# First feed-forward product of a transformer block: one 512-column matmul for two 256-column ones in five of seven block products

## The chip, the cores and the metric

The kernel runs on one core of one Trainium2 chip. A core has TensorE (PE: matmuls, which write to the accumulator memory PSUM), VectorE (DVE), ScalarE (ACT), GpSimd (POOL) and SyncE (SP, which here issues the DMA transfers). Each engine works through its own instructions in order, and semaphores make one wait for another. The metric is the device time of one execution in microseconds (us). Differences under about 0.2% can't be told from none.

## The reference, cut to what matters

One layer: a mixed attention block (8 stick-breaking and 8 forgetting heads), then a feed-forward block with a squared ReLU. 512 tokens, model width 2048, feed-forward width 8192, all float32.

```python
x = x + jnp.einsum('bse,ed->bsd', mixed, w_out[l])

h2 = rmsnorm(x, g_mlp[l])
u = jax.nn.relu(jnp.einsum('bsd,df->bsf', h2, w_up[l]))
x = x + jnp.einsum('bsf,fd->bsd', u * u, w_down[l])
return rmsnorm(x, g_final)
```

The change is in the first of the two feed-forward products, `h2 @ w_up`.

## The kernel before, in words

**Precision.** TensorE multiplies in a reduced float32 form (`fp32r` in the profile). To get full precision every operand is split into a high and a low part (`split`, L69 to L76: ScalarE casts the high part, VectorE subtracts it from the source to get the low part), and a product is three matmuls that add up in PSUM (`mm3`, L103): high x high, high x low, low x high.

**Seven products in place of eight.** The large products are done by Strassen's scheme in Winograd's form: both operands are cut in two by two blocks, and seven products of sums of blocks (numbered 1 to 7) replace eight. For the first feed-forward product the left operand is the normalised residual, whose seven sums are made once and kept in SBUF as `F[p]` (high and low part of each; `f_parts`, L507, gives the two parts of chunk `a`, each 128 x 256: 128 of the inner dimension by 256 tokens). In one tile of `F` the high part lies 4 x 256 elements ahead of the low part.

**Units.** `w_up` is worked through in 32 units of 256 columns (`NU` = 32; class `Unit`, L536). A unit loads its two halves of the rows, 1 MB each (`load`, L548, tag `rw`). For each product `parts` (L554) makes the sum of weight blocks that this product needs (one VectorE subtraction over 128x1024 for products 5, 6, 4, 7: L557 to L563) and splits it into `hi` and `lo`. The buffers for these (`hi_lo`, L80) go round: three from one pool and one more in this stage, so at most four products' weights are held. `multiply` (L568) runs over 8 chunks `a` (order `PAIRS`): three matmuls of 128x128 stationary weights and 256 moving columns each, 24 a product and 168 a unit.

**Accumulators.** A unit has three PSUM tiles, `A`, `B`, `C` (`psa`, `psb`, `psc` in the profile), each of the size of a bank, 512 columns, of which it uses 256, in two sets that the units use in turn. Products 1, 6, 7 and 4 add up in `A` one after the other, 5 and 3 in `C`, 2 is alone in `B`. After 1, 6 and 7 ScalarE copies `A` to SBUF (`m`, L592), and VectorE adds such a copy and `B` or `C` into a quarter of the hidden tile `c` (L598 after 7, L600 after 2, L604 after 3); after 4 ScalarE copies `A` straight into `c` (L602). After 3 the whole `c` goes through Relu and Square (L605, L606).

**Order.** Units 0 and 1 are run product by product at the end of the stage before (L886 to L906). For the rest the loop at L925 interleaves the new unit with the products 4 and 3 of the one before:

```python
        for i, (who, p) in enumerate(((new, 1), (old, 4), (new, 5), (new, 6), (old, 3), (new, 2), (new, 7))):
            if who is None:
                continue
            who.product(p)
            if todo and i in (0, 2, 4, 5):
                store_form(*todo.pop(0))
```

`store_form` (L797) makes one of the seven sums of the hidden values of two units, splits it (tile `st`) and stores it to DRAM (`ufd`): seven of them for each pair of units. They are the left operand of the second feed-forward product (`second`, L840; tile `accd`), which runs 512-column matmuls. A scheduler, which estimates times when the program is built, decides from this order and the dependencies how instructions stand on each engine. In the built program before, TensorE runs 6, 2 and 7 of a unit, then 1 of the next, then 4 of the old one, then 5 of the next.

Of the kernel before, what the change touches and what calls it, by code (L numbers as in the profile page):

```python
# [8 lines left out]
F32 = mybir.dt.float32  # L9
F32R = mybir.dt.float32r  # L10
AF = mybir.ActivationFunctionType
ALU = mybir.AluOpType
PSUM = bass.MemoryType.PSUM

P = 128
NT = 512
# [19 lines left out]
def block_kernel(ctx, tc, x, g_attn, w_in, b_f, g_out_sb, g_out_fox, w_out, g_mlp, w_up, w_down, g_final, y):  # L36
    nc = tc.nc
    pe, act, dve, pool, sp = nc.tensor, nc.scalar, nc.vector, nc.gpsimd, nc.sync
# [64 lines left out]
    def mm3(out, sh, sl, mh, ml, first, last):  # L103
        pe.matmul(out, sh, mh, start=first, stop=False, skip_group_check=True)  # L104
        pe.matmul(out, sh, ml, start=False, stop=False, skip_group_check=True)  # L105
        return pe.matmul(out, sl, mh, start=False, stop=last, skip_group_check=True)  # L106
# [59 lines left out]
    with tc.tile_pool(name="att", bufs=1, side="right", reuse_waits="tile") as at:  # L166
# [15 lines left out]
        def accumulate_v(c0, m, steps, prepare=None, more=None, pool_=None):  # L182

            per = NT // m
            banks = [(acc if pool_ is None else pool_).tile([P, NT], F32, tag="acc", name="accv")
                     for _ in range(2 if more is not None else TB // per)]
            if more is not None:
                banks += [more.tile([P, NT], F32, tag="more", name="accm") for _ in range(2)]
            ps = [banks[t // per][:, t % per * m:(t % per + 1) * m] for t in range(TB)]
            k1 = 0  # L190
            for step in steps:
                k0, k1 = k1, k1 + step
                if prepare is not None:
                    prepare(k0, step)
                w = load_w([w_in[k0 * P:(k0 + step) * P, c:c + m // len(c0)].rearrange("(a p) c -> p a c", p=P) for c in c0],
                           step, m)
                for t in range(TB):
                    ts = slice(t * P, (t + 1) * P)
                    for i in range(step):
                        k = k0 + i  # L200
                        mm3(ps[t], hH[k][:, ts], hL[k][:, ts], *w[i], k == 0 and t % per == 0, k == KC - 1)
            return ps
# [126 lines left out]
        def v_columns(h):  # L329
            return 2 * WSB + h * P if h < NH else o0 + 2 * WSB + (h - NH) * P  # L330

        with tc.tile_pool(name="tr0", bufs=2, space=PSUM) as trp:
# [36 lines left out]
            ps = accumulate_v([v_columns(order[0])], 2 * P + NH, [1, 1] + [2] * 7, prepare, trp)  # L369
# [25 lines left out]
        with tc.tile_pool(name="attp", bufs=1, space=PSUM, reuse_waits="tile") as atp:  # L395
# [18 lines left out]
            for t in range(TB):  # L414
                for i in range(t + 1):
                    pe.matmul(cps[:, t, :], utri if i == t else onesr, lf[:, i, :], start=(t == 0 and i == 0),
                              stop=(i == t), skip_group_check=True)
# [32 lines left out]
            for n in range(0, 2 * NH, 2):  # L450
# [15 lines left out]
                if n == 2 * NH - 2:  # L466
                    ps = accumulate_v([v_columns(order[n])], 2 * P, [4] * 4, pool_=accs[1])
                    with tc.high_priority():
                        vs = take_v(ps)
                elif n % 4 == 2:  # L470
                    c = [v_columns(order[n + i]) for i in (0, 2)]
# [33 lines left out]
    F = {p: [None, None] for p in A_ORDER}  # L505

    def f_parts(p, a):  # L507

        t_ = F[p][a // 2 % 2]
        return [t_[:, c, a // 4 * 2 + a % 2, :] for c in range(2)]  # L510


    PAIRS = (0, 1, 4, 5, 6, 7, 2, 3)
# [22 lines left out]
    class Unit:  # L536
        def __init__(self, u):
            self.u = u
            cols = slice(2 * u * P, 2 * (u + 1) * P)
            rows_ = w_up.rearrange("(a i p) f -> i p a f", i=2, p=P)  # L540
            self.rows = rows_[0][:, :, cols], rows_[1][:, :, cols]
            self.b = []
            if u >= 2:
                self.load(0)
                self.load(1)
            self.A = None

        def load(self, i, a=slice(0, KC // 2)):  # L548
            if a.start == 0:
                self.raw = rw.tile([P, KC // 2, 2 * P], F32, tag="rw", name="wu")  # L550
                self.b.append([self.raw[:, :, j * P:(j + 1) * P] for j in range(2)])
            sp.dma_start(self.raw[:, a], self.rows[i][:, a])
# [15 lines left out]
        def multiply(self, p, parts):  # L568
            hi, lo = parts
            if self.A is None:  # L570
                self.A, self.C, self.B = (ups.tile([P, NT], F32, tag=c, name=f"ps{c}")[:, :2 * P] for c in "acb")
            ps = {1: self.A, 6: self.A, 7: self.A, 4: self.A, 2: self.B, 5: self.C, 3: self.C}[p]
            for a in PAIRS:
                ins = mm3(ps, hi[:, a, :], lo[:, a, :], *f_parts(p, a), a == PAIRS[0] and p in (1, 2, 5), a == PAIRS[-1])
            return ins

        def product(self, p):
            ins = self.multiply(p, self.parts(p))
            self.finish(p)
            return ins  # L580

        def finish(self, p):
            if p == 2:
                if self.u % 2 == 0:
                    hidden[0] = (sg[0].tile([P, 2, 2, NT], F32, tag="c", name="c", bufs=2) if self.u else
                                 rw.tile([P, 2, 2, NT], F32, tag="rw", name="c"))
                self.pair = hidden[0]
                self.c = hidden[0][:, self.u % 2]
            t1, t2 = slice(0, 2 * P), slice(2 * P, NT)
            if p in (1, 6, 7):  # L590
                self.m = sm.tile([P, 2 * P], F32, tag="m6" if p == 6 else "m", name=f"s{p}", bufs=2 if p == 6 else 1)
                act.copy(self.m, self.A)  # L592
                if p == 6:
                    self.m6 = self.m
                if p == 1:
                    self.m1 = self.m
            if p == 7:
                dve.tensor_tensor(self.c[:, 1, t2], self.m, self.C, op=ALU.add)  # L598
            if p == 2:
                dve.tensor_tensor(self.c[:, 0, t1], self.m1, self.B, op=ALU.add)  # L600
            if p == 4:
                act.copy(self.c[:, 0, t2], self.A)  # L602
            if p == 3:
                dve.tensor_tensor(self.c[:, 1, t1], self.m6, self.C, op=ALU.add)  # L604
                act.activation(self.c, self.c, AF.Relu)  # L605
                act.activation(self.c, self.c, AF.Square)  # L606
# [19 lines left out]
    def out_piece(p, db, m0):  # L626

        hi, lo = (w.rearrange("p (a b) -> p a b", a=2) for w in hi_lo(2 * NT))
        if db == 0 and p in (1, 2):
            begun_ = [sp.dma_start(w.bitcast(F32), wraws[p - 1][:, m0 // 2, i]) for i, w in enumerate((hi, lo))][1]  # L630
        elif db == 0 and p == 6:
            begun_ = sp.dma_start(hi.bitcast(F32), whigh[:, m0 // 2])
            sp.dma_start(lo.bitcast(F32), wsums[:, m0 // 2, 3, db])
        else:
            raw = out_weights(p, db, m0)
            casts[0] = split(hi, lo, raw[0])
            begun_ = raw[1]
        ps = {2: B[db], 5: C, 3: C}.get(p, A[db])
        for t in range(2):
            ts = slice(t * P, (t + 1) * P)  # L640
            for i in range(2):
                mm3(ps[:, t, :], G[p][0][:, m0 + i, ts], G[p][1][:, m0 + i, ts], hi[:, i, :], lo[:, i, :],
                    m0 + i == 4 and p in (1, 5, 2), m0 + i == 3)
        return begun_
# [59 lines left out]
    for db in range(2):  # L704
# [25 lines left out]
        for i, p in enumerate(G_ORDER):  # L730
            for m0 in (2,) if db == 0 and p in (1, 2) else (4, 6, 0, 2):
                ins = out_piece(p, db, m0)
                if (db or p in (3, 4)) and m0 in (6, 2) and first_loads:

                    with tc.issue_after(ins.ins):
                        u, k, a = first_loads.pop(0)
# [9 lines left out]
            if db == 0 and p == 5:  # L746
# [3 lines left out]
                rw = ctx.enter_context(tc.tile_pool(name="rw", bufs=5, side="right", reuse_waits="tile"))  # L750
# [37 lines left out]
    ups = ups_cm.__enter__()  # L788
# [34 lines left out]
    def load_uf(p, group):  # L823
        uf[p] = form.tile([P, 2, group[1], 2 * P], F32R, tag=f"fh{UF_AT[p]}", name=f"uf{p}")
        sp.dma_start(uf[p].bitcast(F32), ufd[group][p])
# [55 lines left out]
    hidden = {}  # L881
    todo, sg = [], []
    old = None


    ins = units[0].multiply(1, begun[0])  # L886
# [5 lines left out]
    for p in (1, 2):  # L892
        ins = units[1].product(p)
    left_form(4, 1, 0)
    left_form(5, 1, 0)
    for p in (5, 6, 7, 4, 3):
        for j in range(2):

            with tc.issue_after(ins.ins):
                ins = units[j].product(p)  # L900
# [24 lines left out]
    for u in range(2, NU + 1):  # L925
        new = None if u == NU else Unit(u)
        if u == NU - 1:
            for p in ORDER:
                load_uf(p, GROUPS[0])
            b_first = load_b(GROUPS[0], 0)  # L930
        if new is None:
            second(1, b_first, 0, GROUPS[0][1], True)
        for i, (who, p) in enumerate(((new, 1), (old, 4), (new, 5), (new, 6), (old, 3), (new, 2), (new, 7))):
            if who is None:
                continue
            who.product(p)
            if todo and i in (0, 2, 4, 5):
                store_form(*todo.pop(0))
            if p == 3 and who.u % 2 == 1 and who.u < NU - 2:
                todo += [(q, who.pair, who.u - 1) for q in A_ORDER]  # L940
        old = new
# [153 lines left out]
    for t in range(2, TB):  # L1095
        for n in range(4):
            ins = last_product(t, n, *banks[n % 2])
# [31 lines left out]
```

## Time and profile before

| | us |
|---|---|
| median of 3 runs (lowest, highest) | 2068.32 (2067.92, 2069.01) |
| the profiled execution's own time | 2068.49 |
| its span, first to last instruction | 2066.8 |
| first `psa` matmul to last (units 0 to 31) | 793.5 to 1442.6 |
| first `st` cast to last (hidden values stored) | 841.3 to 1437.7 |

The profile comes from one execution. Its page gives busy time of each engine, and groups of instructions by source line, engine, output and inputs, with their count, their summed and mean duration, and the idle time of the engine ahead of them with what ended it. `PEld` is the load of stationary weights, which overlaps matmuls. Further views show instructions in order of time, waits (who waited for whom, with the sum, how often and the longest), and busy time in stretches of the span. In a group line `L106 PE MATMUL psa<-f,wl 128*128 128x256 f32` means: source line 106, TensorE, a matmul into `psa` from `f` (moving) and `wl` (stationary 128*128), 256 columns wide.

### The profile page before, as it was taken

To read this page: it belongs to the slowest core of one execution; us is meant where nothing else is said; L and a number is where in the kernel's file an instruction comes from. 1 tells how busy PE (TensorE), PEld (TensorE's weight loads), DVE (VectorE), ACT (ScalarE), POOL (GpSimd) and SP (SyncE) were. 2 spreads that over 40 slices of the span, in tenths; PEclk is the share of its full clock that TensorE was granted. 3 is DMA by queue.
4 is the path that set the end of the run, shared out by engine and by line. 5 is a ranking of instruction groups with operands and counts; after the bars stand their busy time and mean duration, and the time that the engine had idled before them with its cause. 6 is when DMAs were issued, how large, how long until landed. Compare 5 with 4: busy or idle time off the path is not lost.

```text
span 2066.8 us, 29903 instructions
## 1 busy us (share of the span) xinstructions
PE 2048.8 (99%) x12000; PEld 1822.3 (88%) x12000; DVE 1614.3 (78%) x1772; ACT 1050.8 (51%) x1428; POOL 55.3 (3%) x76
## 2 busy tenths in 40 slices
PE   9999999999999999999999999999999999999998
PEld 8888888888898889999999999999888888888886
DVE  6677754657578588888888888888788888989895
ACT  6444433454455556666656666666743444433434
POOL 0000000000000000000000000000000000000003
PEclk9999999999999999999999999999999999999999
DMA  7888742323337872666666666576855764763732
GB/s 247 295 295 276 234 130 73 83 82 82 82 108 266 294 265 87 198 190 187 213 193 188 195 209 194 180 217 247 306 201 195 261 239 158 278 241 135 274 112 82
DMA packets 258859, 402.60 MB, mean 195 GB/s; under 512 B 9456, under 2 KB 154912, under 8 KB 251168
## 3 DMA queue, kind: packets, MB, share of 16 engines
q1 hardware_dynamic: 257760, 398.56, 57.7%
q8 instruction: 94, 1.54, 0.3%
q10 hardware_dynamic: 960, 2.13, 0.3%
q14 instruction: 45, 0.37, 0.0%
HBM read 307.85 MB, written 92.80 MB: 194 GB/s over the span
## 4 chain that ended last, share of the span: by engine, by line
PE 92%; DVE 5%; DMA 1%; issue 1%; ACT 1%; POOL 0%; SPq 0%; ACTq 0%; DVEq 0%
PE accd L104 7%; PE accd L106 7%; PE accd L105 7%; PE psa L106 6%; PE psa L104 6%; PE psa L105 6%; PE accq L105 6%; PE accq L104 6%; PE accq L106 6%; PE psc L104 3%; PE psc L106 3%; PE psc L105 3%; PE accv L104 2%; PE accv L105 2%; PE accv L106 2%; PE psb L106 1%
## 5 line engine op out<-in xcount | busy, mean ns | idle before, releaser
L71 ACT CAST wh<-wu 128x1024 fp32r<-128x1024 f32 x171 | 178.1, 1048 | 132.8 <-PE psa L105 54.2
L72 DVE TENSOR_TENSOR wl<-wu,wh 128x1024 fp32r<-128x1024 f32 x171 | 208.1, 1221 | 44.4 <-ACT wh L71 43.2
L71 ACT CAST wh<-wd 128x1024 fp32r<-128x1024 f32 (+1 forms) x136 | 134.8, 1000 | 183.5 <-PE accd L106 112.6
L106 PE MATMUL psa<-f,wl 128*128 128x256 f32 x792 | 224.2, 283 | 1.3 <-DVE wl L72 1.3
L105 PE MATMUL psa<-f,wh 128*128 128x256 f32 x792 | 224.1, 283 | 0.0
L104 PE MATMUL psa<-f,wh 128*128 128x256 f32 x792 | 224.1, 283 | 0.0
L104 PE MATMUL accq<-hH,wh 128*128 128x512 f32 x512 | 200.4, 391 | 0.4 <-DVE vl L75 0.4
L106 PE MATMUL accq<-hH,wl 128*128 128x512 f32 x512 | 200.2, 391 | 0.0
L105 PE MATMUL accq<-hL,wh 128*128 128x512 f32 x512 | 200.2, 391 | 0.0
L72 DVE TENSOR_TENSOR wl<-wd,wh 128x1024 fp32r<-128x1024 f32 (+1 forms) x136 | 155.4, 1154 | 36.4 <-ACT wh L71 35.9
L104 PE MATMUL accd<-wh,uf 128*128 128x512 f32 x436 | 169.7, 389 | 1.0 <-issue 1.0
L106 PE MATMUL accd<-wh,uf 128*128 128x512 f32 x436 | 169.6, 389 | 0.0
L105 PE MATMUL accd<-wl,uf 128*128 128x512 f32 x436 | 169.6, 389 | 0.0
L72 DVE TENSOR_TENSOR wl<-wraw,wh 128x1024 fp32r<-128x1024 f32 (+2 forms) x101 | 119.6, 1185 | 61.3 <-ACT wh L71 55.6
L71 ACT CAST wh<-wraw 128x1024 fp32r<-128x1024 f32 (+2 forms) x101 | 101.9, 1009 | 119.9 <-PE accq L105 70.6
L106 PEld LDWEIGHTS psa<-f,wl 128*128 128x128 f32 x792 | 152.0, 192 | 1.5 <-DVE wl L72 1.5
L104 PEld LDWEIGHTS psa<-f,wh 128*128 128x128 f32 x792 | 152.1, 192 | 0.1
L105 PEld LDWEIGHTS psa<-f,wh 128*128 128x128 f32 x792 | 152.0, 192 | 0.1
L71 ACT CAST wx<-wd 128x1024 fp32r<-128x1024 f32 (+1 forms) x88 | 87.4, 999 | 114.7 <-PE accd L106 72.7
L72 DVE TENSOR_TENSOR wx<-wd,wx 128x1024 fp32r<-128x1024 f32 (+1 forms) x88 | 101.0, 1154 | 23.7 <-ACT wx L71 23.4
L104 PEld LDWEIGHTS accq<-hH,wh 128*128 128x128 f32 x512 | 96.1, 188 | 20.2 <-PE accv L106 0.8
L106 PEld LDWEIGHTS accq<-hH,wl 128*128 128x128 f32 x512 | 96.2, 188 | 19.3
(346 smaller groups left out, 5553.5 us busy)
## 6 DMA issues: line engine op xcount, KB each, us to landing
wu<-in_w_up_dram SPq DMA_DIRECT2D x60, 1024.0 KB, 6.8
ufd<-st SPq DMA_DIRECT2D x98, 512.0 KB, 7.0
wd<-in_w_down_dram SPq DMA_DIRECT2D x48, 1024.0 KB, 5.9
wraw<-in_w_in_dram SPq DMA_DIRECT2D x84, 512.0 KB, 3.8
uf<-ufd SPq DMA_DIRECT2D x42, 1024.0 KB, 5.6
mixed<-in_w_out_dram SPq DMA_DIRECT2D x8, 2048.0 KB, 7.7
wsums<-mixed SPq DMA_DIRECT2D x8, 2048.0 KB, 7.3
wo<-wsums SPq DMA_DIRECT2D x28, 512.0 KB, 4.4
```

Of the source, the lines that this page charges most:

```text
L71: ins = act.copy(hi, src)
L72: lows[0] = dve.tensor_tensor(lo, src, hi.bitcast(F32), op=ALU.subtract)
L104: pe.matmul(out, sh, mh, start=first, stop=False, skip_group_check=True)
L105: pe.matmul(out, sh, ml, start=False, stop=False, skip_group_check=True)
L106: return pe.matmul(out, sl, mh, start=False, stop=last, skip_group_check=True)
```

## The change

For units 2 and up (`self.both`), products 1, 6, 7, 4 and 2 are multiplied in another way. The high weights of a chunk meet the high and the low part of the left operand in one matmul of 2 x 256 columns: high x high goes to the first half of the accumulator's bank, high x low to the second half. A second matmul of 256 columns adds low x high to the second half. So the five products have 2 matmuls a chunk in place of 3. Products 5 and 3 stay as they were.

`A` and `B` now have two halves that are to be added. ScalarE copies `A` after product 1 into `B`, all 512 columns, and product 2 then adds onto it. After 6, 2, 7 and 4 ScalarE copies the first half into `c` and the second into a new tile `l` of the same shape (one buffer). VectorE adds `C` to `c` after 7 and after 3, and after 3 adds the whole of `l` to the whole of `c` (128x1024), ahead of Relu and Square. `sm` tiles and the three adds of before are no longer used by these units.

In units 0 and 1 product 2 gets one more 256-column matmul, into the unused half of `B`'s bank, which starts the accumulation there.

In the loop old product 3 comes ahead of new product 6. In the built program TensorE then runs 6 and 2 of a unit, 1 of the next, 7 of the unit, 5 of the next, 4 and 3 of the old one, and then 6 of the next.

```diff
--- before.py
+++ after.py
@@ -544,6 +544,7 @@
                 self.load(0)
                 self.load(1)
             self.A = None
+            self.both = u >= 2
 
         def load(self, i, a=slice(0, KC // 2)):
             if a.start == 0:
@@ -568,10 +569,25 @@
         def multiply(self, p, parts):
             hi, lo = parts
             if self.A is None:
-                self.A, self.C, self.B = (ups.tile([P, NT], F32, tag=c, name=f"ps{c}")[:, :2 * P] for c in "acb")
+                self.A, self.C, self.B = (ups.tile([P, NT], F32, tag=c, name=f"ps{c}") for c in "acb")
+                self.C, self.rest = self.C[:, :2 * P], self.B[:, 2 * P:]
+                if not self.both:
+                    self.A, self.B = self.A[:, :2 * P], self.B[:, :2 * P]
             ps = {1: self.A, 6: self.A, 7: self.A, 4: self.A, 2: self.B, 5: self.C, 3: self.C}[p]
+            if self.both and p not in (5, 3):
+
+
+                ps = ps.rearrange("p (c n) -> p c n", c=2)
+                for a in PAIRS:
+                    t_ = F[p][a // 2 % 2][:, :, a // 4 * 2 + a % 2, :]
+                    pe.matmul(ps, hi[:, a, :], t_, start=a == PAIRS[0] and p == 1, stop=False, skip_group_check=True)
+                    ins = pe.matmul(ps[:, 1], lo[:, a, :], t_[:, 0], start=False, stop=a == PAIRS[-1], skip_group_check=True)
+                return ins
+            if p == 2:
+
+                pe.matmul(self.rest, hi[:, 0, :], f_parts(p, PAIRS[0])[0], start=True, stop=True, skip_group_check=True)
             for a in PAIRS:
-                ins = mm3(ps, hi[:, a, :], lo[:, a, :], *f_parts(p, a), a == PAIRS[0] and p in (1, 2, 5), a == PAIRS[-1])
+                ins = mm3(ps, hi[:, a, :], lo[:, a, :], *f_parts(p, a), a == PAIRS[0] and p in (1, 5), a == PAIRS[-1])
             return ins
 
         def product(self, p):
@@ -579,11 +595,35 @@
             self.finish(p)
             return ins
 
+        def finish_both(self, p):
+            if p == 6:
+                if self.u % 2 == 0:
+                    hidden[0] = sg[0].tile([P, 2, 2, NT], F32, tag="c", name="c", bufs=2)
+                self.pair = hidden[0]
+                self.c = hidden[0][:, self.u % 2]
+                self.l = sg[0].tile([P, 2, NT], F32, tag="l", name="l")
+            t1, t2 = slice(0, 2 * P), slice(2 * P, NT)
+            if p == 1:
+                act.copy(self.B, self.A)
+            at_ = {6: (1, t1), 2: (0, t1), 7: (1, t2), 4: (0, t2)}.get(p)
+            if at_ is not None:
+                ps = self.B if p == 2 else self.A
+                act.copy(self.c[:, at_[0], at_[1]], ps[:, :2 * P])
+                act.copy(self.l[:, at_[0], at_[1]], ps[:, 2 * P:])
+            if p in (7, 3):
+                c = self.c[:, 1, t2 if p == 7 else t1]
+                dve.tensor_tensor(c, c, self.C, op=ALU.add)
+            if p == 3:
+                dve.tensor_tensor(self.c, self.c, self.l, op=ALU.add)
+                act.activation(self.c, self.c, AF.Relu)
+                act.activation(self.c, self.c, AF.Square)
+
         def finish(self, p):
+            if self.both:
+                return self.finish_both(p)
             if p == 2:
                 if self.u % 2 == 0:
-                    hidden[0] = (sg[0].tile([P, 2, 2, NT], F32, tag="c", name="c", bufs=2) if self.u else
-                                 rw.tile([P, 2, 2, NT], F32, tag="rw", name="c"))
+                    hidden[0] = rw.tile([P, 2, 2, NT], F32, tag="rw", name="c")
                 self.pair = hidden[0]
                 self.c = hidden[0][:, self.u % 2]
             t1, t2 = slice(0, 2 * P), slice(2 * P, NT)
@@ -930,7 +970,7 @@
             b_first = load_b(GROUPS[0], 0)
         if new is None:
             second(1, b_first, 0, GROUPS[0][1], True)
-        for i, (who, p) in enumerate(((new, 1), (old, 4), (new, 5), (new, 6), (old, 3), (new, 2), (new, 7))):
+        for i, (who, p) in enumerate(((new, 1), (old, 4), (new, 5), (old, 3), (new, 6), (new, 2), (new, 7))):
             if who is None:
                 continue
             who.product(p)
```

## The prediction

> **What bounds the kernel now.** I read the page from the top: the share of each engine, the granted clock, the chain that ended last.
>
> ```profile
> span 2066.8 us, 29903 instructions
> PE 2048.8 (99%) x12000; PEld 1822.3 (88%) x12000; DVE 1614.3 (78%) x1772; ACT 1050.8 (51%) x1428; POOL 55.3 (3%) x76
> PEclk9999999999999999999999999999999999999999
> PE 92%; DVE 5%; DMA 1%; issue 1%; ACT 1%; POOL 0%; SPq 0%; ACTq 0%; DVEq 0%
> ```
>
> TensorE is never idle for long, its clock is granted in full, and 92% of the last chain is matmuls. A shorter matmul stream therefore shortens the kernel, as long as the other engines keep feeding it. Whether they do is read in the stage that changes, the first feed-forward product (units 2 to 31, about 840 to 1448 us). Next, the windows view, busy time per engine in six stretches:
>
> ```profile
> core 0: us, PE busy (x) PEld busy (x) DVE busy (x) ACT busy (x) POOL busy (x), PEclk, DMA share, GB/s
> 868.00:1436.00 568.00, 567.75 (x4730) 567.50 (x4730) 483.17 (x546) 344.52 (x463) 0.00 (x0) 1.00 0.62 197
> 888.00:908.00 20.00, 20.00 (x169) 20.00 (x168) 18.50 (x24) 12.61 (x19) 0.00 (x0) 1.00 0.63 185
> 990.00:1030.00 40.00, 39.75 (x331) 39.55 (x330) 36.57 (x41) 26.84 (x35) 0.00 (x0) 1.00 0.61 188
> 1420.00:1440.00 20.00, 20.00 (x153) 19.28 (x152) 16.60 (x20) 12.33 (x18) 0.00 (x0) 1.00 1.03 381
> 1440.00:1460.00 20.00, 20.00 (x112) 17.53 (x112) 16.55 (x19) 15.40 (x20) 0.00 (x0) 1.00 0.95 333
> 1700.00:1800.00 100.00, 100.00 (x443) 82.77 (x442) 90.07 (x67) 40.82 (x41) 0.00 (x0) 1.00 0.61 226
> ```
>
> In 568 us TensorE misses 0.25 us, while VectorE is at 85% and ScalarE at 61%. VectorE is the next bound. The second product (last row) has TensorE at 100%, so time won earlier is kept to the end.
>
> **What a matmul costs.** The 283 ns that the page gives for a 256-column matmul is its latency; they are pipelined, so what counts is the distance between two starts. From TensorE's timeline come the first and last of 24 consecutive 256-column matmuls, the first and last of 15 consecutive 512-column ones (second product), and, near the end, the one place where a 512 is followed by 256s:
>
> ```profile
> 1101.65 0.28 PE L104 MATMUL psa<-f,wh 128*128 128x256 f32 x1
> ...
> 1104.41 0.28 PE L106 MATMUL psa<-f,wl 128*128 128x256 f32 x1
> ```
> ```profile
> 1699.81 0.39 PE L104 MATMUL accd<-wh,uf 128*128 128x512 f32 x1
> ...
> 1702.98 0.39 PE L106 MATMUL accd<-wh,uf 128*128 128x512 f32 x1
> ```
> ```profile
> 2055.05 0.39 PE L106 MATMUL acce<-ws,us 128*128 128x512 f32 x1
> 2055.28 0.28 PE L104 MATMUL acce<-ws,us 128*128 128x256 f32 x1
> 2055.39 0.28 PE L105 MATMUL acce<-ws,us 128*128 128x256 f32 x1
> ```
>
> 2.76 us over 23 steps is 120.0 ns; 3.17 us over 14 steps is 226.4 ns. The step from 512 to 256 takes 0.23 us and the next 0.11 to 0.12, so mixing adds nothing visible. The two pitches together give 0.416 ns a column and about 13.6 ns for each matmul whatever its width. The change removes instructions, not columns, so what it can win is this fixed part.
>
> **The change, part by part.** (1) *Fewer matmuls.* Before, a unit has 7 products x 8 chunks x 3 matmuls of 256 columns: 168 x 120.0 = 20.16 us. In five products each chunk becomes one 512 and one 256: 226.4 + 120.0 = 346.4 ns in place of 360.0. A unit then takes 40 x 346.4 + 48 x 120.0 = 19.62 us, 0.54 us less. Over 30 units (2 to 31) this is 40 x 30 x 13.6 ns = 16.3 us. Two extra 256-column matmuls, one in each of units 0 and 1, give back 0.24 us. The two built programs agree: TensorE has 1198 matmuls fewer. The bounds of the unseen step: the 512 reads its columns as two runs of 256 that lie apart, which no row shows. At worst it costs two 256s (240.0 ns), and the whole gain is gone; at best it is the 226.4 of the row. I take the row: its width, output and type are the same, only the read address jumps once.
>
> [...]
>
> (2) *VectorE and ScalarE.* The groups of the stage between 868 and 1436 us, and the one copy of 1024 columns out of PSUM from a later stretch:
>
> ```profile
> L72 DVE TENSOR_TENSOR wl<-wu,wh 128x1024 fp32r<-128x1024 f32 x145 | 176.4, 1221 | 38.3 <-ACT wh L71 37.2 <-PE psc L106 0.8
> L72 DVE TENSOR_TENSOR st<-c,st 128x512 fp32r<-128x512 f32 x97 | 64.2, 686 | 20.0 <-ACT st L71 19.7
> L561 DVE TENSOR_TENSOR wu<-wu 128x1024 f32<-128x1024 f32 x28 | 34.2, 1222 | 0.5
> L600 DVE TENSOR_TENSOR c<-s,psb 128x256 f32<-128x256 f32 x29 | 12.0, 414 | 0.0
> L598 DVE TENSOR_TENSOR c<-s,psc 128x256 f32<-128x256 f32 x28 | 11.6, 415 | 0.9 <-ACT s L592 0.9
> ```
> ```profile
> L71 ACT CAST wh<-wu 128x1024 fp32r<-128x1024 f32 x146 | 152.2, 1048 | 115.6 <-PE psa L105 44.6 <-PE psc L105 37.1 <-DVE wu L559 12.9
> L592 ACT COPY s<-psa 128x256 f32<-128x256 f32 x84 | 30.9, 368 | 40.0 <-PE psa L106 38.6 <-DVE c L598 1.4
> L602 ACT COPY c<-psa 128x256 f32<-128x256 f32 x28 | 10.3, 369 | 3.8 <-PE psa L106 3.8
> L605 ACT ACTIVATE c<-c 128x1024 f32<-128x1024 f32 x28 | 29.6, 1058 | 4.0 <-DVE c L604 3.6
> ```
> ```profile
> L866 ACT COPY m<-accd 128x1024 f32<-128x1024 f32 x12 | 12.1, 1012 | 5.8 <-PE accd L106 5.7
> ```
>
> VectorE loses three adds of 0.415 us per unit and gets two of these and one over 128x1024 (1.22 us, by the equal form of L561): +0.81 us. It was busy 483.17 us in 568/20.16 = 28.2 units, 17.15 us a unit; it becomes 17.95 of 19.62 us, 91.5%. Its idle time falls from 3.0 to 1.66 us a unit. ScalarE has four copies of 0.368 us now; it gets eight, plus one 512-column copy from PSUM to PSUM. That copy's price lies between 0.37 (256 columns) and 1.01 us (1024); by the columns 0.58. So +2.05 us: from 12.23 to 14.3 us a unit, 73%. All of this is hidden behind matmuls while both engines stay ahead; without that cover it costs 0.81 + 2.05 us in each unit.
>
> (3) *What queues behind.* The five evacuations on ScalarE each wait for the end of a product, and the casts of the next weights stand behind them. The low halves are held in one buffer, so the copy of product 6's low half waits for the big add of the unit before. In the built order of the fullest unit, VectorE does after the old product 3: add 0.41, weight sum 1.22, low part for the store 0.69, A sum 0.69, split 1.22, big add 1.22; then ScalarE does its Relu (1.06) and the copy (0.37): about 6.9 us. Product 7, which writes the same bank again, may start after products 6, 2 and the next unit's 1: 3 x 8 x 346.4 ns = 8.3 us. Slack 1.4 us. From 7 to 4 lies product 5, 24 x 120.0 ns = 2.88 us, against two copies of 0.37 us and a cast of 1.05 that may stand ahead: slack 1.1 us. Both hold on average, but a late VectorE eats them. The price: before, in its fullest 40 us (36.57, 91.4%), TensorE lost 0.25 us, that is 0.125 us a unit. The new average is such a load, so 30 x 0.125 = 3.8 us; bounds 0 and the whole gain and more (rival 2).
>
> (4) *Moved.* Old product 3 comes ahead of new product 6. No DMA is added; the stores of the split hidden values keep their number and places in the loop, and with the loads share a DMA load of 0.62. At the stage's end DMA is at 0.95 to 1.03 and TensorE still loses nothing (rows 1420 and 1440). The last unit hands its PSUM banks over one copy later: 0.4 us at most, within the 3.8.
>
> **Sum.** 2068.49 (the profiled execution's time; span 2066.8 plus 1.7 around it; the median of the runs is 0.17 lower) - 16.3 + 0.24 + 3.8 = 2056.2, or **2056.0** against the median.
>
> **Rivals.** The waits of the stage show how much idle VectorE has been made to take:
>
> ```profile
> ACT st L71 <- DMA ufd<-st: 42.0, 26, 4.2
> DVE wl L72 <- ACT wh L71: 37.4, 50, 1.7
> DVE wx L72 <- ACT wx L71: 23.5, 21, 2.6
> DVE st L72 <- ACT st L71: 19.7, 16, 3.1
> PE psc L104 <- ACT wh L71: 0.3, 1, 0.3
> ```
>
> *Rival 1, half kept.* VectorE falls behind once in every pair of units (its stores come in bursts) and TensorE waits 0.15 to 0.4 us a unit: 2052.3 + 30 x 0.15..0.4 = 2057 to 2064. For it: the 888 window, 18.50 of 20 busy before the extra 0.81. Against: no wait there at all.
>
> *Rival 2, slower: VectorE sets the pace.* Its idle before is nearly all waiting for a cast by ScalarE, which itself waits for TensorE to free a weight buffer or for a store to land (42.0 us). If all 3.0 us a unit are forced by this loop, a unit lasts 17.95 + 3.0 = 20.95 us, 0.79 more than now: 2068.3 + 30 x 0.79 = 2092. It decides from 2.2 us of forced idle a unit (20.16 - 17.95). Against: where VectorE had 1.5 us idle in 20 (888 window), TensorE lost nothing, and a cast that waits for a buffer is early, not late. Centre 2080.
>
> *Rival 3, the change doesn't do what it says:* the 512 with two runs costs 240 ns, gain nil, and 0.24 plus 3.8 us are added: 2072. For it stands only that no row shows the form. [...]
>
> **How the numbers follow.** Forecast (2052 to 2057) 0.48, rival 1 (2057 to 2064) 0.25, rival 3 (2066 to 2072, no change) 0.09, rival 2 (from 2073) 0.18. Below about 2064 is faster by more than 0.2% (4.1 us), which is what a measurement can tell here: 0.73 faster, 0.09 same, 0.18 slower. The range 2051.5 to 2073 leaves out rival 2 and little else; the forecast's own range, rival 1 included, is 2051.5 to 2064.
>
> **What would show it.** Right: in the changed stage, starts 226 ns apart after a 512 and 120 after a 256, and some 19.6 to 19.8 us a unit; VectorE at 90 to 93% there, ScalarE near 73%; TensorE's waits in the stage a few us, for a split or for a copy of psa; the second product unchanged in length. Wrong: a 512 pitch near 240 (rival 3); or TensorE busy well under 99% in the stage, with waits on VectorE's splits or on ScalarE's copies of more than 0.5 us in each unit (rival 2).

## The result, and the profile after

The changed kernel took 2074.01 us (median of 9 runs, 2073.06 to 2075.52), the kernel before 2069.01 on the same chip (9 runs, 2067.21 to 2069.43): ratio 1.0027, 95% interval 1.0017 to 1.0037. A fall of about 13 us was forecast; the time rose by 5.0. The profiled spans say the same, 2071.7 against 2066.8 (+4.9). Of all executions reported here one, of the experiment with high weights first in all seven products, took 5273.38 us; its ratio leaves that one out. The top of the page of the changed kernel:

```profile
span 2071.7 us, 27664 instructions
PE 2045.1 (99%) x10802; PEld 1758.9 (85%) x10802; DVE 1639.4 (79%) x1772; ACT 1089.8 (53%) x1578; POOL 55.2 (3%) x76
PE 89%; DVE 5%; DMA 3%; ACT 2%; issue 1%; SPq 0%; POOL 0%; ACTq 0%; DVEq 0%
```

The 1198 matmuls are gone, and yet the span is longer. In the chain that ended last, matmuls have 89% in place of 92%, DMA and ScalarE 5% together in place of 2%. The windows view of the changed kernel has the same columns as in the prediction: busy time and instructions of each engine, granted clock, DMA share, GB/s.

```profile
868.00:1436.00 568.00, 559.97 (x3579) 504.17 (x3578) 505.66 (x545) 380.31 (x600) 0.00 (x0) 1.00 0.61 196
868.00:1430.00 562.00, 553.97 (x3543) 498.82 (x3542) 499.66 (x537) 376.38 (x594) 0.00 (x0) 1.00 0.61 196
1700.00:1800.00 100.00, 100.00 (x443) 82.84 (x442) 88.21 (x67) 41.22 (x41) 0.00 (x0) 1.00 0.67 245
```

In the 568 us of the prediction's first row TensorE now misses 8.0 us; it missed 0.25. VectorE is at 89%, ScalarE at 67%. The second product (last row) is as it was. So the loss is in the changed stage. Its waits on TensorE (868 to 1430 us; total, times, longest), and the waits themselves on TensorE's timeline (start, duration, in brackets the idle time ahead and who ended it):

```profile
PE psc L106 <- DVE wl L72: 4.4, 7, 0.8
PE psa L583 <- ACT l L612: 3.0, 6, 0.5
PE psc L104 <- ACT wh L71: 0.5, 1, 0.5
```
```profile
913.86 0.39 PE L106 MATMUL psc<-f,wl 128*128 128x256 f32 x1 [0.67 <-DVE wl L72]
954.41 0.50 PE L583 MATMUL psa<-f,wh 128*128 128x512 f32 x1 [0.50 <-ACT l L612]
...
1105.49 0.40 PE L583 MATMUL psa<-f,wh 128*128 128x512 f32 x1
1105.72 0.28 PE L584 MATMUL psa<-f,wl 128*128 128x256 f32 x1
...
1108.32 0.40 PE L583 MATMUL psb<-f,wh 128*128 128x512 f32 x1
...
1116.80 0.28 PE L104 MATMUL psc<-f,wh 128*128 128x256 f32 x1
1116.92 0.28 PE L105 MATMUL psc<-f,wh 128*128 128x256 f32 x1
1117.70 0.50 PE L583 MATMUL psa<-f,wh 128*128 128x512 f32 x1 [0.50 <-ACT l L612]
1118.04 0.28 PE L584 MATMUL psa<-f,wl 128*128 128x256 f32 x1
...
1402.56 0.39 PE L106 MATMUL psc<-f,wl 128*128 128x256 f32 x1 [0.75 <-DVE wl L72]
```

Two kinds of wait take turns, each once in four units. Seven times the low weights of product 5 (`wl`) are late: VectorE has not split them when TensorE has done its first two matmuls. (In three of the seven the high weights are late as well.) Six times product 4 stands in TensorE's queue after only *two* matmuls of product 5 (1116.80 and 1116.92, then `psa`), so the two copies that empty `psa` after product 7 have 0.24 us of cover, where the prediction counted on the whole of product 5, 2.88 us.

A bracket undercounts, because the page gives the matmul before it a modelled end: from 1116.92 to 1117.70 are 0.78 us where 0.12 is usual, and the next step is 0.1 long too, so the wait of 0.50 costs 0.77. I call this excess of start-to-start distances a gap. Over the stage and its end (830 to 1460 us) the gaps sum to 13.2 us: 7.7 late weights of product 5 (6.3 low, 1.4 high), 6 x 0.77 = 4.6 before product 4, 1.0 at the stage's end. Before, one gap of 0.5 us stood there.

The second loss is in the pairs. From 1105.49 to 1108.32 run 8 pairs in 2.83 us, 353.7 ns each, where 346.4 were expected. Over all starts of 1000 to 1200 us a 512 followed by a 256 takes 236.5 ns (395 of them), a 256 followed by a 512 117.1: 353.6 a pair. The account, all against the profiled execution of before: -16.3 (removed matmuls) + 0.24 (two extra) + 1200 x 7.2 ns = 8.6 (pairs) + 12.7 (gaps, 13.2 less the 0.5 of before) = +5.2 us; measured +4.9.

How weights come late is seen once on ScalarE's and VectorE's timelines, ahead of the wait at 1077.16:

```profile
1068.19 1.06 ACT L71 CAST wx<-wu 128x1024 fp32r<-128x1024 f32 x1
1070.74 0.37 ACT L611 COPY c<-psb 128x256 f32<-128x256 f32 x1 [1.49 <-PE psb L584]
1071.01 1.06 ACT L618 ACTIVATE c<-c 128x1024 f32<-128x1024 f32 x1
1071.97 0.36 ACT L612 COPY l<-psa 128x256 f32<-128x256 f32 x1
1072.22 0.39 ACT L612 COPY l<-psb 128x256 f32<-128x256 f32 x1
1073.33 0.62 ACT L71 CAST st<-c 128x512 fp32r<-128x512 f32 x1 [0.73 <-DMA ufd<-st]
1073.86 1.05 ACT L619 ACTIVATE c<-c 128x1024 f32<-128x1024 f32 x1
1074.82 1.98 ACT L71 CAST wh<-wu 128x1024 fp32r<-128x1024 f32 x2
```
```profile
1075.88 2.36 DVE L72 TENSOR_TENSOR wl<-wu,wh 128x1024 fp32r<-128x1024 f32 x2 [1.21 <-ACT wh L71]
```

Between one cast and the next stand a wait of 1.49 us for the end of product 2, Relu, two copies that wait their turn, a store's cast that waits for a DMA, and Square. The cast of product 5's weights starts at 1074.82; VectorE has idled 1.21 us for it when it starts at 1075.88. So VectorE is late here because ScalarE is, and ScalarE is late because of what stands ahead in its queue, with a third of its time idle on average. Relu itself doesn't idle for the big add here. Where it does, on ScalarE's waits of the same stretch (868 to 1430 us), is another unit of the four, and TensorE loses nothing there:

```profile
ACT c L618 <- DVE c L617: 5.1, 7, 0.7
```

### The profile page after: what moved, and what is told of

Same layout as the page of the kernel before. It is cut to its first block, busy times and chain, and to the rows that moved or that the text cites. A ratio compares the mean times of both kernels' runs of the same rounds, so it can differ in the third digit from the quotient of the medians.

```text
span 2071.7 us, 27664 instructions
## 1 busy us (share of the span) xinstructions
PE 2045.1 (99%) x10802; PEld 1758.9 (85%) x10802; DVE 1639.4 (79%) x1772; ACT 1089.8 (53%) x1578; POOL 55.2 (3%) x76
## 4 chain that ended last, share of the span: by engine, by line
PE 89%; DVE 5%; DMA 3%; ACT 2%; issue 1%; SPq 0%; POOL 0%; ACTq 0%; DVEq 0%
PE psa L583 9%; PE accd L104 7%; PE accd L105 7%; PE accd L106 7%; PE accq L105 6%; PE accq L106 6%; PE accq L104 6%; PE psa L584 5%; PE psc L106 3%; PE psc L104 3%; PE psc L105 3%; PE accv L104 2%; PE accv L105 2%; PE accv L106 2%; DMA ufd<-st 2%; PE psb L583 2%
## 5 line engine op out<-in xcount | busy, mean ns | idle before, releaser
L583 PE MATMUL psa<-f,wh 128*128 128x512 f32 x728 | 261.3, 400 | 3.7 <-ACT l L612 3.7
L584 PE MATMUL psa<-f,wl 128*128 128x256 f32 x728 | 204.4, 281 | 0.0
L583 PEld LDWEIGHTS psa<-f,wh 128*128 128x128 f32 x728 | 136.9, 188 | 36.7 <-ACT l L612 5.3
L584 PEld LDWEIGHTS psa<-f,wl 128*128 128x128 f32 x728 | 137.7, 189 | 0.1
L106 PE MATMUL psc<-f,wl 128*128 128x256 f32 x384 | 109.3, 285 | 4.4 <-DVE wl L72 4.4
L105 PEld LDWEIGHTS accq<-hL,wh 128*128 128x128 f32 x512 | 96.2, 188 | 19.2
```

Of the source, the lines that this page charges most:

```text
L583: pe.matmul(ps, hi[:, a, :], t_, start=a == PAIRS[0] and p == 1, stop=False, skip_group_check=True)
L584: ins = pe.matmul(ps[:, 1], lo[:, a, :], t_[:, 0], start=False, stop=a == PAIRS[-1], skip_group_check=True)
```

## The experiments

Each is the changed kernel with the edit shown. Labels such as e6, which the expectations use, stand with the name of the kernel. "Gaps" are counted as above. A caveat for all of them: the order of each engine's queue is made anew for every kernel, so an edit moves more than its own lines. Kernels listed together ran beside the same runs of before, whose medians were 2070.04 (23 runs), 2069.18 (28), 2069.48 (7) and 2068.47 us (15) in the four batches.

### First batch: is it the address of the 512, product 4, or VectorE's add?

**Left parts adjacent (e1).** The two runs of 256 columns lie side by side, so the 512 reads one run.

```diff
-            F[p][db] = form.tile([P, 2, 4, 2 * P], F32R, ...)
+            F[p][db] = form.tile([P, 4, 2, 2 * P], F32R, ...).rearrange("p a c n -> p c a n")
```

> The high and low part of a chunk of the left operand now lie side by side, so a 512-column matmul reads one run of 512 in place of two runs of 256; the order on TensorE is that of the changed kernel. Theory 'two runs cost': a 512 and a 256 together fall from 353 to 346 ns, 1200 pairs give 8 us, the time is about 2066. Rival 'the mix of widths costs': the pair stays at 353 ns and the time at 2074. In both the waits (13 us in gaps) stay as they are, within 2 us.

2075.69 us (8 runs), ratio 1.003 (1.0019 to 1.004). The timeline of this kernel, first and last of nine 512s:

```profile
1105.33 0.40 PE L583 MATMUL psa<-f,wh 128*128 128x512 f32 x1
...
1108.17 0.40 PE L583 MATMUL psb<-f,wh 128*128 128x512 f32 x1
```

8 pairs in 2.84 us: 236.4 and 117.2 ns over all starts of 1000 to 1200 us, as with two runs. The two runs cost nothing, and the mechanism of rival 3 falls. What is left for the 7 ns is the turn between widths itself, which the second batch takes up.

**Product 4 after the whole of product 5 (e2).**

```diff
+            if p == 4 and who.both and new is not None:
+                late = who.parts(4)
+                continue
-            who.product(p)
+            last = who.product(p)
+            if p == 5 and old is not None and old.both:
+                with tc.issue_after(last.ins):
+                    old.multiply(4, late)
+                old.finish(4)
```

> Old product 4 may start only after the whole of new product 5, in every unit. In the changed kernel it came after two matmuls of product 5 in every second unit, and waited 0.77 us there for the two copies of psa. Theory 'no cover for the copies': these 7 gaps go, 5 to 6 us less, about 2068.5; the other 7 gaps, on product 5's low part, stay. Rival 'late weights': the gap moves to product 5's low part in the same units, and the time stays at 2073 to 2075.

2072.24 us (10 runs), 1.0015 (1.0006 to 1.0024). The waits for the copies of `psa` are gone; the late weights grew in their place (waits on TensorE of this kernel):

```profile
PE psc L106 <- DVE wl L72: 5.2, 7, 0.8
PE psc L104 <- ACT wh L71: 1.8, 3, 1.0
```

Gaps 13.2 us: mending one wait alone passes most of it on. This profile is of the slowest of the ten executions (2076.41 us), and 1.5 us of its gaps are matmuls at half clock: after waits of 0.99 and 0.75 us on TensorE in the same product the granted clock is 0.57 from 1243 to 1247 us. (The expectation puts product 4 after two matmuls of product 5 in every second unit; the trace of the changed kernel has it in one of four.)

**No big add (e4).** The add of the low halves, `self.c + self.l`, is left out (its copies stay).

```diff
-                dve.tensor_tensor(self.c, self.c, self.l, op=ALU.add)
```

> The big add of the low half (128x1024 on VectorE, once in a unit) is left out, so the output lacks high x low and low x high of five products; the copies on ScalarE stay. VectorE falls from about 18.0 to 16.8 us a unit, below what it had before. Theory 'VectorE is too full': nearly all 13 us of gaps go, about 2061. Rival 'ScalarE's queue': Relu starts earlier, but product 5's cast still stands behind the copies, half of the gaps stay, about 2067 or more.

2060.12 us (4 runs), 0.995 (0.9933 to 0.9966); no gaps. Without this add they are all gone: is it its 1.22 us of VectorE, or who waits for it?

**Big add earlier (e5),** after product 4 in place of product 3.

```diff
-            if p == 3:
+            if p == 4:
                 dve.tensor_tensor(self.c, self.c, self.l, op=ALU.add)
+            if p == 3:
                 act.activation(self.c, self.c, AF.Relu)
```

> The big add comes after product 4 instead of after product 3: the same work on every engine, but Relu waits only for the small add after product 3, and the low buffer is free one product (2.9 us) earlier. Theory 'ScalarE's queue' (Relu and Square wait for the big add with the casts behind them): gaps fall from 13 to under 7 us, about 2067. Rival 'VectorE is too full': no change, 2072 to 2075.

2072.3 us (10 runs), 1.0011 (1.0002 to 1.0021). The work of every engine is the same, yet in the stage only some 3 us of gaps are left, and no low weights are late. But at its end a new wait stands. TensorE's and ScalarE's timelines there, and the windows around it:

```profile
1456.91 0.39 PE L106 MATMUL accd<-wh,uf 128*128 128x512 f32 x1
1462.77 0.79 PE L104 MATMUL accd<-wh,uf 128*128 128x512 f32 x1 [5.47 <-ACT m L907]
```
```profile
1459.96 0.72 ACT L917 ACTIVATE xr<-xr,v 128x512 f32<-128x512 f32 x1 [6.16 <-DMA xr<-xd]
```
```profile
1456.00:1462.00 6.00, 1.30 (x6) 0.75 (x4) 0.69 (x1) 2.04 (x4) 0.00 (x0) 0.83 0.97 264
1462.00:1467.00 5.00, 4.23 (x10) 3.36 (x11) 1.92 (x2) 5.00 (x8) 0.00 (x0) 0.52 0.80 289
```

ScalarE stands 6.16 us before an operation whose data has not landed; the copy `m<-accd` that TensorE needs is queued behind it. After the pause the granted clock is 0.52 for about 4 us, and a 512 takes 0.4 us to the next instead of 0.23. Together some 8 us go there; with two shorter waits just ahead, first to last `accd` matmul take 584.2 us, against 574.9 in the changed kernel. (Other runs here show slow clock after shorter pauses: e2 above, 0.57 granted after 0.99 and 0.75 us; e9 below, 0.56 granted from 1436.2 to 1440 us after 2.2 us.)

### Second batch: grouping by width, and the add's work against the wait for it

**High weights first in the five products (e6):** eight 512s, then eight 256s, one change of width in place of sixteen, and low weights needed 1.8 us later.

```diff
                     pe.matmul(ps, hi[:, a, :], t_, ...)
+                for a in PAIRS:
+                    t_ = F[p][a // 2 % 2][:, :, a // 4 * 2 + a % 2, :]
                     ins = pe.matmul(ps[:, 1], lo[:, a, :], t_[:, 0], ...)
```

> In the five products, all 8 matmuls of the high weights come first and then all 8 of the low weights, so the widths change once in a product in place of sixteen times. Theory 'the mix of widths costs 6.7 ns a pair': the 512s go to 226.6 ns and the 256s to 120.0, 7 of 8 of the 7.8 us come back, about 2067 if the gaps (13 us) stay. Rival 'the 512 itself costs 6.7 ns more here': no change of the pitch, 2074. A low part that comes late costs less in these products, but the gaps stand at product 5, which is left as it is.

2066.77 us (10 runs), 0.9991 (0.9981 to 1.0). The timeline of this kernel:

```profile
1056.16 2.00 PE L583 MATMUL psa<-f,wh 128*128 128x512 f32 x8
1058.00 1.11 PE L586 MATMUL psa<-f,wl 128*128 128x256 f32 x8
1058.95 0.40 PE L583 MATMUL psa<-f,wx 128*128 128x512 f32 x1
```

A product takes 2.79 us against 2.83 in turn, and 2.77 by the prediction's two pitches: about two thirds of the 7 ns are won back. The rest stands at the head of each row of 512s. By the medians of this kernel's starts the steps behind the first five 512s of a product take 233, 236, 228, 233 and 231 ns, those behind the last three 227, the pitch of the second product, although these too read two runs. So a turn of widths is felt for about five matmuls, and neither the 512 nor its two runs is dearer for good. The late weights are gone but for 0.4 us once; the six waits before product 4 stay (3.0 us idle), and a wait with slow clock at the stage's end comes in as in the kernel with the early add (3.1 us of wait; granted clock 0.96 on average from 1430 to 1470 us, 1.00 in the changed kernel). That the time is the 2067 of the expectation is partly luck: it had kept all gaps, but the late weights went and the loss at the end came in.

**Small add (e7):** the big add takes every 8th column only, so its order stays and its length shrinks.

```diff
-                dve.tensor_tensor(self.c, self.c, self.l, op=ALU.add)
+                dve.tensor_tensor(self.c[:, :, ::8], self.c[:, :, ::8], self.l[:, :, ::8], op=ALU.add)
```

> The big add takes every eighth column only (128x128 elements in place of 128x1024), so most of the low half is missing from the output; what waits for it is as before. VectorE has about 1.0 us less work a unit. Theory 'work on VectorE': the gaps go as without the add, about 2060 to 2061. Rival 'the wait for the add after product 3': the copies of the next unit's product 6 and Relu still wait for it, so that 4 us or more of gaps remain, 2064 or more.

2063.02 us (7 runs), 0.9971 (0.996 to 0.9982); gaps 1.2, of which 1.0 at the stage's end. That ScalarE has to wait for an add is not enough; its length counts.

**The same length, with nobody waiting (e10):** the big add is left out, and an add of equal length on a weight block stands after product 7's weights. The block is used once more: product 4's weight sum is formed from it, so product 4's weights are not the scheme's.

```diff
+            if p == 7 and self.both:
+                dve.tensor_tensor(b11, b11, b12, op=ALU.add)
-                dve.tensor_tensor(self.c, self.c, self.l, op=ALU.add)
```

> Without the big add (the low half is missing from the output), but with a dead add of the same size on VectorE over a weight block that is used up: the work of the changed kernel, with nothing waiting for it but the next load of weights. Theory 'work on VectorE': 10 us or more of gaps, 2071 to 2075. Rival 'the wait for the add': gaps under 3 us, 2060 to 2063.

2065.28 us (10 runs), 0.9979 (0.997 to 0.9988). Windows and waits on TensorE of this kernel:

```profile
868.00:1430.00 562.00, 558.49 (x3592) 505.52 (x3591) 498.17 (x547) 387.19 (x605) 0.00 (x0) 1.00 0.63 200
```
```profile
PE psa L585 <- ACT l L614: 3.5, 7, 0.5
```

VectorE is as busy as in the changed kernel (498.17 against 499.66 us) and no weights are late; only product 4 waits, 7 x 0.77 = 5.4 us. With the run before: neither the work alone nor the wait alone makes weights late. A long add in that place does, though not by Relu waiting for it, as the waits of the changed kernel showed; how it does is taken up with the fourth batch.

**High weights first in all seven products (e9)** (products 5 and 3 too).

> High weights first in all seven products of units 2 and up: the first low part is needed 1.8 to 1.9 us later than before. Theory 'the low part of product 5 comes late (gaps of 0.9 us)': those gaps go and the pairs are 346.6 ns; about 2060 if the wait of product 4 for the copies of psa stays, 2054 if it goes too. Rival 'lateness only moves': gaps of the same sum stand at other products, 2066 to 2068.

2069.81 us (10 runs), 1.0001 (0.9991 to 1.0011). TensorE now waits for `wh` at the first matmul of product 5 or 3 (5.1 us, 6 times), and 2.2 and 1.7 us at the stage's end: the lateness moved.

### Third batch: the add on GpSimd

Four kernels with `pool.tensor_tensor` for the big add: alone (e11); with high weights first in the five products (e12); as e12, with product 4 after product 5 too (e13); as e12, with high weights first in all products (e14).

> The big add runs on GpSimd, which is otherwise idle in this stage, in the place and with the waits that it has in the changed kernel. VectorE keeps less work than before the change. An add of 128x1024 on GpSimd should take about 2.6 us (its 128x512 multiply took 1.30). Theory 'VectorE must not be in the chain from product 3 to Relu': gaps under 3 us, about 2061. Rival 'any wait for the add holds ScalarE': the add is now slower, gaps of 8 us or more, 2069 or more. In both the pair of a 512 and a 256 stays at 353 ns.

> As the last one, with the high weights first in the five products. If the mix of widths (7 us) and the gaps are separate losses, both go: about 2054. If not, no better than the better of the two alone, 2060 or more.

> As e12, with old product 4 held behind the whole of new product 5. If what is left of gaps is the wait for the copies of psa, they go and the time falls by up to 3 us below e12; if that order already covers the copies, the same as e12.

> As e12, with the high weights first in products 5 and 3 too, so a low part that comes late costs less there. If late low parts are what is left, 1 to 3 us below e12; if not, the same.

2082.72 us, 1.0068 (1.0053 to 1.0083); 2079.57, 1.0049 (1.0034 to 1.0064); 2097.01, 1.0142 (1.0118 to 1.0165); 2118.58, 1.023 (1.0187 to 1.0274); 4 runs each. GpSimd's add takes 2.7 us in the first (3.0, 3.4 and 4.5 on average in the others), and VectorE isn't relieved: 513.83 us busy in 868 to 1430 us against 499.66. The timelines of the first of them:

```profile
1072.85 2.40 POOL L617 TENSOR_TENSOR c<-c,l 128x1024 f32<-128x1024 f32 x1 [20.11 <-DVE c L615]
```
```profile
1073.25 2.55 DVE L72 TENSOR_TENSOR st<-c,st 128x512 fp32r<-128x512 f32 x1 [0.54 <-ACT st L71]
```

VectorE's low part for the store takes 0.69 us by itself; begun during GpSimd's add, it ends 0.55 us after it. Moving the add there costs VectorE more than it saves (14.2 us more busy time), and Relu waits for an add of 2.7 us in place of 1.22. In e13 and e14 TensorE's largest wait is for the copies of `psa` (10.9 and 27.8 us, 868 to 1430 us); why it grows so much there was not followed.

### Fourth batch: ScalarE's queue

**No Square (e15).** The Square after the Relu is left out in units 2 and up: ScalarE loses 1.05 us a unit ahead of the cast, VectorE nothing.

```diff
-                act.activation(self.c, self.c, AF.Square)
```

> Square is left out in units 2 and up (the hidden values stay unsquared): ScalarE has 1.06 us less a unit, just ahead of the cast for product 5; VectorE's work and the big add are as in the changed kernel. Theory 'ScalarE's queue': the gaps on product 5's weights go (8 of 13 us), 2066 or less. Rival 'VectorE itself is late': they stay, 2072 to 2075.

2070.73 us (10 runs), 1.0009 (1.0 to 1.0018). Windows, waits on TensorE, and the timeline at the stage's end:

```profile
868.00:1430.00 562.00, 558.99 (x3590) 505.46 (x3588) 504.99 (x547) 358.46 (x575) 0.00 (x0) 1.00 0.62 200
```
```profile
PE psa L583 <- ACT l L612: 3.0, 6, 0.5
```
```profile
1439.81 0.80 PE L583 MATMUL psa<-f,wh 128*128 128x512 f32 x1 [3.41 <-ACT l L612]
```

In the stage no weights are late any more, with VectorE *busier* than in the changed kernel (504.99 against 499.66 us in 562). So it is ScalarE's queue that makes them late. But it is not only the 1.05 us of Square, for the order changed too. The same place in the queue as in the changed kernel's timeline above:

```profile
1066.02 1.05 ACT L71 CAST wx<-wu 128x1024 fp32r<-128x1024 f32 x1
1066.97 1.06 ACT L618 ACTIVATE c<-c 128x1024 f32<-128x1024 f32 x1
1067.93 0.36 ACT L612 COPY l<-psa 128x256 f32<-128x256 f32 x1
1068.58 0.37 ACT L611 COPY c<-psb 128x256 f32<-128x256 f32 x1 [0.29 <-PE psb L584]
```

Relu now stands ahead of the copy of product 2's result, which waits 0.29 us in place of 1.49, and the cast of `wh` starts at 1069.11, 2.0 us after the end of this cast in place of 5.6. The kernel with the small add has the same order of Relu and copy, and a distance of 3.0 us. So the late weights go with the order that the scheduler gave ScalarE's queue. That it chose the worse one because of the add's length is likely, and not shown. The total misses what was expected, because at the end of the stage a wait of 3.41 us with about 5 us of slow clock takes the gain (the 512 at 1439.81 takes 0.60 us to the next start in place of 0.24).

**A clean end, then an early add, then product 4 late (e16, e17, e18).** Three kernels, each with the edits of the one before. The first has high weights first in the five products and, in the second product, the store work and the residual (`xr<-xd`) behind the cast of the weights in ScalarE's queue; the second has the early add too; the third also the whole of product 5 ahead of product 4.

```diff
-            split(hi, lo, src[:, u0:u0 + m, :])
+            casts[0] = split(hi, lo, src[:, u0:u0 + m, :])
...
-                    jobs.pop(0)()
+                    with tc.issue_after(casts[0].ins):
+                        jobs.pop(0)()
...
-                    add_residual(*pieces.pop(0))
+                    with tc.issue_after(casts[0].ins):
+                        add_residual(*pieces.pop(0))
```

> High weights first in the five products, and the casts of the last hidden values and the scaling of the residual may not go ahead of the second product's casts on ScalarE. The loss at the stage's end (3 us of waiting and some 3 us of halved clock with e6) goes: about 2061, against 2066.8 for e6. If it only moves, 2065 or more.

> As e16, with the big add after product 4 in place of 3. With the early add alone the gaps within the stage were about 3 us: 2057 if the parts add up, 2061 or more if not.

> As e17, with old product 4 held behind the whole of new product 5. About 2055 if the last gaps are the wait for the copies of psa; 2058 or more if holding it back makes other weights late.

2062.0 us (6 runs), 0.9968 (0.9956 to 0.9981), with the six waits before product 4 as the only waits in its stage; 2055.7 (4 runs), 0.9939 (0.9924 to 0.9954), 0.2 us of gaps; 2054.15 (4 runs, 2054.12 to 2054.83), 0.9931 (0.9916 to 0.9946), no gaps. From first to last `accd` matmul the three take 574.5 to 574.8 us (574.6 before), so the whole gain lies in the changed stage. The stage of the last in the windows view:

```profile
868.00:1430.00 562.00, 562.00 (x3644) 514.18 (x3643) 512.56 (x553) 390.17 (x611) 0.00 (x0) 1.00 0.64 206
```

TensorE misses nothing in 562 us, with VectorE at 91.2%, the load that the prediction reckoned with (91.5%), and above the 88.9% at which the changed kernel lost its 12 us. This version beats both kernels, by 14.3 us that of before. The last step, from 2055.7 to 2054.15, is smaller than the intervals of the two ratios can part.

## Why the forecast missed, by its own steps

*(1) Fewer matmuls.* The mechanism was right, and a term of it too large. 1198 matmuls fell away, 256s alone still stand 120.0 ns apart, and the two runs cost nothing (adjacent columns: the same pitch). But the pair of 512 and 256 takes 353.6 ns, not 226.4 + 120.0: the gain is 6.4 ns a pair, and 1200 pairs won 7.7 us where 16.3 were put down. By the prediction's own sign the reading is mixed: 236.5 ns after a 512 is near rival 3's 240, but the 256 behind it takes 117. "Mixing adds nothing visible" rested on one turn of widths, with 0.23 and 0.11 us given to hundredths: too coarse for 7 ns that are taken 1200 times. Grouping by width won about two thirds of it back, and the rest falls on the first five 512s after a turn; why a turn costs this is open.

*(2) VectorE and ScalarE.* The sizes of the single operations hold. The groups of the changed kernel (868 to 1430 us):

```profile
L617 DVE TENSOR_TENSOR c<-c,l 128x1024 f32<-128x1024 f32 x27 | 32.9, 1219 | 0.3
L607 ACT COPY psb<-psa 128x512 f32<-128x512 f32 x28 | 16.5, 588 | 0.0
```

1.219 us for the add (1.22 was taken) and 0.588 for the copy (0.58). VectorE came to 88.9% rather than 91.5 because a unit became longer, not shorter: from 913.86 to 1402.56 are 24 units of 20.36 us, against 20.16 before and 19.6 to 19.8 forecast. ScalarE's 67% has a second reason: 67% of 20.36 is 13.6 us a unit, where 14.3 were forecast. The sum added full durations, but copies that follow another operation start about 0.1 us before its end (1071.97 and 1072.22 in the timeline above).

*(3) What queues behind.* This step failed: 3.8 us were put down, 12.7 measured (the 1.0 at the stage's end among it). The price came from VectorE's average load (0.125 us a unit at 91%), and load is not what decides: with the same VectorE work in another place no weights were late, without Square none were late at a higher load, and at 91.2% in a better order nothing was lost. The slack of 1.1 us between products 7 and 4 assumed that product 5 lies between them, as the order given under "The change" has it; the built order has two of its 24 matmuls there in one unit of four. The slack of 1.4 us was reckoned for the copy of product 6's low half; what in fact came late was the cast of product 5's weights, behind Relu, Square, a store's cast and the copies with their waits in ScalarE's queue, a step that the prediction had named ("the casts of the next weights stand behind them") but not followed to its end.

*(4) Moved,* and the stage's end: 1.0 us against 0.4, small here. But in four of the experiments the end took back the gain of the stage, up to 9 us with the slow clock. That DMA at 0.95 to 1.03 cost TensorE nothing before was no promise for another order in ScalarE's queue. That the stage ends earlier isn't the reason: the first `accd` matmul starts at 1445.6 us before, at 1442.8 with the early add, which loses most there, and at 1438.8 without the big add, which loses nothing.

*The rivals.* Rival 1 came nearest: VectorE behind in bursts, in part of the units. Its price was 0.15 to 0.4 us a unit; measured are 12.7 / 30 = 0.42, and half of the pitch's gain was missing besides. Rival 2 (VectorE sets the pace) isn't shown, although the sign is its own: TensorE's waits are in one unit of two, not in each, and the load of VectorE could rise without any. Rival 3 named the right row to doubt, the 512, for the wrong reason.

## What to carry to other kernels

When work is moved to an engine that is not the bound, read the built order of its queue around each instruction that the bound engine waits for, and count what stands ahead of it, waits included; the average load says little, since here 89% stalled and 91% did not. A gain of some nanoseconds an instruction that is taken a thousand times needs the pitch of the very sequence that will run, over many steps. And let the end of a stage be part of the sum: a new order there can put an operation that waits for a transfer ahead of the copy that TensorE needs, 6.16 us in one kernel here.

## What the runs showed of the hardware

- A matmul of 512 columns followed by one of 256 took 236.5 ns to the next start and the 256 after it 117.1, 7 ns a pair above the pitches of each width by itself (226.4 and 120.0); eight and eight in a row took 2.79 us in place of 2.83, and there only the first five 512s stood more than 227 ns apart.
- A moving operand in two runs of 256 columns cost nothing against 512 adjacent ones (353.6 ns a pair with either).
- A wait of TensorE with 0.50 us in its bracket cost 0.77 in start-to-start distance (product 4 in the changed kernel).
- After a pause of 5.6 us TensorE ran for about 4 us at a granted clock of 0.52 (e5); in other runs the granted clock was 0.56 after a pause of 2.2 us (e9), and 0.57 after two of 0.99 and 0.75 us within one product (e2).
- A VectorE operation of 0.69 us, begun during GpSimd's add, took 2.55 and ended 0.55 us after that add (e11).
